# Weight splits ahead of evacuations in the second projection, a residual loaded in four parts, spreading products with 128 rows, a last store from ScalarE: a hybrid mLSTM and stick-breaking layer on one Trainium2 core

## The chip, the cores and the metric

The kernel runs on one core of one Trainium2 chip. The time is the device time of one execution in microseconds (us), the median of several runs. A profile is one execution taken by the hardware profiler; its span goes from the first to the last instruction of the program, and its engines are TensorE (PE; its weight loads are PEld), VectorE (DVE), ScalarE (ACT), GpSimd (POOL) and SyncE (SP). An engine's name with a q (SPq) is its sequencer, which issues transfers and waits for semaphores.

## The reference

One layer over 512 tokens of width 1024, in float32:

```python
h = rmsnorm(x, norm_w)
proj = h @ w_in + b_in            # 1024 -> 11272 columns, split into the parts below
# A: mLSTM, 4 heads of 256: causal conv + SiLU on q and k, matrix memory with gates, per-head norm
y_m = norm(mlstm(mq, mk, mv, mi, mf)) * sigmoid(mo) * silu(mz)
# B: stick-breaking attention, 8 heads of 128, strictly causal, normed q and k
y_s = stick_breaking(norm(sq), norm(sk), sv) * silu(sz)
merged = sigmoid(gm) * (y_m @ w_proj_m) + sigmoid(gs) * (y_s @ w_proj_s)
out = x + merged @ w_out
```

## The kernel before

Every product of two float32 matrices is made of three TensorE products in a faster format: each operand is split into a high half (rounded) and a low half (the rest), and `mm3` (lines 84 to 87) adds high x high, high x low and low x high. ScalarE makes the high half by a copy (line 90), VectorE the low half by a subtraction (line 91).

The program is a list of units, one after the other on TensorE. A unit of a projection is 128 output columns (or 256 input rows) and 24 products of 512 columns each. In order: the input projection (`w_in`), the projection of `y_s` (`w_proj_s`, 8 units), the projection of `y_m` (`w_proj_m`, 8 units, called the second projection), and then the output product. `n_proj` is the number of the first output unit, so units `n_proj - 8` to `n_proj - 1` are the second projection. The heads of both mixers run between the units of the input projection.

The output product is made by a scheme with seven products of half size (numbered 1, 2, 6, 5, 7, 4, 3, in this order) from sums of blocks of `w_out` (B11, B12, B21, B22; T1 to T4 are their sums) and of `merged` (the tables `s`). Each of the seven is two units of 12 products.

For each unit c the main loop (from line 1141) writes the instructions of all engines; each engine then executes its own in that order and waits for the others by semaphores. `ahead(c)` splits the weights of the units up to c + 2 and has SP load the raw weights of the units up to c + 4 (`fetch`). `evac` of unit c - 1 takes its result out of PSUM. `due` is a list of deferred pieces. In the units up to `n_proj` the evacuation comes first, then the deferred pieces, then `ahead`; behind `n_proj` there is an `ahead` in front of the evacuation.

- For the second projection the split is different (`by_dma`, lines 115 to 119): ScalarE copies the high half into `wh` and minus the high half into `wl`, and then GpSimd issues a DMA that adds the raw weight `stg` onto `wl`. The buffers `stg`, `wh` and `wl` have three places each.
- The evacuation of a unit of the second projection (`pm_evac`, lines 850 to 868) is VectorE's product with the gate and sum with the first projection, then ScalarE's copy to `mgh` and VectorE's `mgl`; from the fifth unit on also four VectorE operations for the tables. The evacuation of the first projection is one VectorE operation (line 845).
- `s_turn` splits a table of sums (ScalarE and VectorE), `t4` makes T4 on VectorE.
- `load_xr` (line 932) has SP load the eight 128x512 pieces of x for the residual. It is a deferred piece at unit `n_proj - 2`.
- `add` (line 971) adds a product onto such a piece on VectorE and stores it by SP; the last piece goes in two halves of 256 columns. `add_dma` adds by a DMA from GpSimd.
- Four times, once for each mLSTM head, TensorE spreads a row over all partitions: line 688 multiplies `sel`, a tile of 36 rows with ones in eight of them, with `rb2`, the row in two halves. Both tiles are cleared by GpSimd at the start (lines 496 and 497), then a few rows are written.

Of the kernel before, what the change touches and what calls it, by code (L numbers as in the profile page):

```python
# [9 lines left out]
FR = mybir.dt.float32r  # L10
# [5 lines left out]
T = 512  # L16
# [18 lines left out]
def tile_hybrid_layer(  # L35
# [16 lines left out]
    nc = tc.nc  # L52
    xf = x.flatten_outer_dims()
    of = out.flatten_outer_dims()

    def pool(name, bufs=1, **k):
        return ctx.enter_context(tc.tile_pool(name=name, bufs=bufs, **k))

    cst = pool("cst")
# [13 lines left out]
    def blk(tag, dt=F32, shape=(512,), name=None, p=128):  # L73

        where = mp if tag in MISC else sp
        return where.tile([p] + list(shape), dt, name=name or tag, tag=tag, bufs=BUFS[tag])
# [193 lines left out]
    def x_scale(tb):  # L270
        xs = tiny.tile([128, 4], F32, name="xs", bufs=2)
        ssq, r = xs[:, 0:2], xs[:, 2:3]
        xn = x_t[tb]
        junk = blk("om", BF, (D,), name="junk")
        if tb == 0:
            for i in range(2):
                c = slice(i * D // 2, (i + 1) * D // 2)
                nc.scalar.activation(junk[:, c], xn[:, c], AF.Square, accum_out=ssq[:, i:i + 1])
            nc.gpsimd.tensor_tensor(ssq[:, 0:1], ssq[:, 0:1], ssq[:, 1:2], op=OP.add)
        else:  # L280
            nc.scalar.activation(junk, xn, AF.Square, accum_out=ssq[:, 0:1])
        rstd(r, ssq[:, 0:1], D, EPS)
        nc.vector.tensor_scalar(xn, xn, r, None, op0=OP.mult)

    def x_turn(tb):
        ts = slice(tb * 128, (tb + 1) * 128)
        xn = x_t[tb]
        for g in range(2):
            ks = slice(4 * g, 4 * g + 4)
            tp = att_ps()  # L290
            for j in range(4):
                kt = g * 4 + j
                nc.tensor.transpose(tp[:, j * 128:(j + 1) * 128], xn[:, kt * 128:(kt + 1) * 128], ident)
            dh = hh[:, ks, ts]
            nc.vector.tensor_tensor(dh, tp.rearrange("p (k t) -> p k t", k=4),
                                    nw_t[:, ks].unsqueeze(2).to_broadcast([128, 4, 128]), op=OP.mult)
            for j in range(4):
                k = 4 * g + j
                nc.vector.scalar_tensor_tensor(hl[:, k, ts], tp[:, j * 128:(j + 1) * 128], nw_t[:, k:k + 1],
                                               hh[:, k, ts].bitcast(F32), op0=OP.mult, op1=OP.subtract)  # L300
# [175 lines left out]


    NH = 4
    sel = cst.tile([36, NH, 128], FR, name="sel")
    rb2 = cst.tile([36, T], FR, name="rb2")  # L480
    c_lag = [cst.tile([128, TB, NH], F32, name=f"c_lag{k}") for k in range(TB)]
    em = cst.tile([128, TB, NH], F32, name="em")
    gst = blk("y", shape=(KT, 8), name="gst")
# [3 lines left out]
    def gates_fill():  # L487
        wg = blk("P5", FR, (KT, 128), name="wg")
        nc.gpsimd.memset(wg.bitcast(F32), 0.0)

        sel32 = blk("y", shape=(NH, 128), name="sel32", p=36)
        nc.gpsimd.memset(sel32, 1.0)
        for r in (slice(0, 4), slice(32, 36)):
            nc.gpsimd.affine_select(out=sel32[r], in_=sel32[r], compare_op=OP.is_equal, fill=0.0, base=0,
                                    channel_multiplier=1, pattern=[[-1, 4], [0, 128]])
        nc.gpsimd.memset(sel.bitcast(F32), 0.0)
        nc.gpsimd.memset(rb2.bitcast(F32), 0.0)
        wg_t.extend([wg, sel32])
# [372 lines left out]
    n_proj = len(units)  # L871
# [58 lines left out]

    xr = {}

    def load_xr():
        for n, (g, tb) in enumerate([(0, 0), (0, 1), (1, 0), (1, 1), (1, 2), (1, 3), (0, 2), (0, 3)]):
            tag = ["om", "om", "om", "acc", "tmp", "tmp", "brow", "vh"][n]
            t = blk(tag, shape=({"om": 516, "vh": 576}.get(tag, 512),), name="xr")[:, 0:512]
            nc.sync.dma_start(t, xf[tb * 128:(tb + 1) * 128, g * 512:(g + 1) * 512])
            xr[g, tb] = t
# [32 lines left out]
    def add(g, tb, src, store=False, n=512):  # L971
        t = xr[g, tb]
        for c in range(0, 512, n):
            nc.vector.tensor_tensor(t[:, c:c + n], src[:, c:c + n], t[:, c:c + n], op=OP.add)
            if store:
                nc.sync.dma_start(of[tb * 128:(tb + 1) * 128, g * 512 + c:g * 512 + c + n], t[:, c:c + n])

    def add_dma(g, tb, src):
        nc.gpsimd.dma_start(out=xr[g, tb], in_=src, accum_op=OP.add)
# [10 lines left out]
    def p2():  # L990
        for tb in range(2):
            add(0, tb, bank[2, tb], True)
# [6 lines left out]
    def p5():  # L999
        for tb in range(2):  # L1000
            add(1, 2 + tb, bank[5, tb])
        for tb in range(2):
            add(1, tb, bank[5, tb])
# [27 lines left out]
    def at(c, fn, *a):  # L1031
        later.setdefault(n_proj + c, []).append(lambda: fn(*a))

    for g in range(2):
# [4 lines left out]
        at(-7 + 2 * g, t2, g)  # L1039
        at(-6 + 2 * g, t1, g)  # L1040
        at(1 + g, t4, g)
    at(-2, load_xr)
    for j in range(4):
        at(j // 2, s_turn, 12, j)
        at(3 + j, s_turn, 34, j)
# [89 lines left out]
    def ahead(c):  # L1135
        while count["ready"] < min(N, c + AHEAD + 1):
            fetch(count["ready"] + 1)
            units[count["ready"]].split()
            count["ready"] += 1
        fetch(c + LOADS + 1)  # L1140

    for c in range(N):
        now[0] = c
        if 0 < c < TB:
            ahead(c)
        if c and units[c - 1].slow:
            units[c - 1].slow()
            ahead(c)
        due = later.pop(c, [])
        if c > n_proj:  # L1150
            ahead(c)
        if c:
            units[c - 1].evac()
        for fn in due:
            fn()
        ahead(c)
        units[c].mm(0)
        if c < 2:
            x_turn(c + 1)
        if c == 0:  # L1160
            x_scale(2)
            x_scale(3)
            gates_fill()
        for g in list(act):
            if c in REST:
                continue
            if next(g, "end") == "end":
                act.remove(g)
        for e in list(pend):
            if c >= e[0] and e[2]():  # L1170
                pend.remove(e)
                g = e[3]()
                next(g)
                act.append(g)
        units[c].mm(1)
        if c == 1:
            x_turn(3)
# [31 lines left out]
```

## Time and profile before

| | |
|---|---|
| median of 3 runs | 716.22 us (715.57 to 717.08) |
| the profiled execution | 716.44 us |
| its span | 714.6 us |
| granted TensorE clock over the span | 0.999 |
| TensorE busy | 704.1 us, 3332 products |
| VectorE busy | 446.5 us |
| ScalarE busy | 335.5 us |
| GpSimd busy | 106.8 us |
| moved by DMA | 73.57 MB, of it the accumulating copies and additions (software queue) 5.77 MB |

Each row of a timeline gives the start and the length of an instruction in us, the engine, the line of the kernel, the operation, the tiles as out<-in, and in brackets the idle time of the engine before it and what ended it. `x2` joins two of the same kind in a row. A row of windows gives, for a stretch, its length, the busy time and count of PE, PEld, DVE, ACT and POOL, then the granted clock, the busy share of the 16 DMA engines, and GB/s.

### The profile page before, as it was taken

How to read it: one execution, taken by the hardware profiler on the slowest of the kernel's cores; microseconds unless marked ns; L12 is line 12 of the kernel's file. 1: busy time of each engine (PE TensorE's matmuls, PEld its weight loads, DVE VectorE, ACT ScalarE, POOL GpSimd, SP SyncE). 2: the span in 40 equal slices, each digit the busy share in tenths (PEclk: the TensorE clock that was granted, in tenths of full speed). 3: DMA queues.
4: the chain of work that ended last, by engine and by line, in shares of the span. 5: the costliest groups of instructions: out<-in, count | busy, mean ns of one | idle time of the engine just before them, and what ended most of it. 6: DMA issues, size and time to landing. Idle time of an engine off the chain costs nothing.

```text
span 714.6 us, 9124 instructions
## 1 busy us (share of the span) xinstructions
PE 704.1 (99%) x3332; PEld 586.6 (82%) x3332; DVE 446.5 (62%) x711; ACT 335.5 (47%) x629; POOL 106.8 (15%) x249
## 2 busy tenths in 40 slices
PE   7999999999999999999999999999999999999997
PEld 5888888888888888888888888888888888887786
DVE  6837886656487567279944637995343254445896
ACT  5245364476255544244475534446563253334451
POOL 5412021253022112000001120000111000111010
PEclk9999999999999999999999999999999999999999
DMA  7433332233323222333332233333323236569244
GB/s 241 133 104 93 99 90 73 69 95 87 105 61 88 59 74 75 103 89 90 93 93 79 59 104 89 89 89 89 89 60 87 76 118 222 146 152 263 87 89 117
DMA packets 93492, 73.57 MB, mean 103 GB/s; under 512 B 3694, under 2 KB 77832, under 8 KB 93448
## 3 DMA queue, kind: packets, MB, share of 16 engines
q1 hardware_dynamic: 91432, 67.23, 32.7%
q0 software_dynamic: 2016, 5.77, 4.3%
q8 instruction: 26, 0.43, 0.2%
q14 instruction: 18, 0.15, 0.1%
HBM read 65.12 MB, written 2.10 MB: 94 GB/s over the span
## 4 chain that ended last, share of the span: by engine, by line
PE 88%; issue 5%; DMA 4%; DVE 1%; POOL 1%; SPq 0%; ACT 0%; DVEq 0%; POOLq 0%
PE dps L85 24%; PE dps L87 24%; PE dps L86 24%; PE aps L86 3%; PE aps L87 3%; PE aps L85 3%; DMA wl<-stg 2%; PE aps L447 1%; PE aps L389 1%; PE dps L1098 1%; PE dps L1096 1%; PE dps L1097 1%; DMA stg<-in_w_in_dram 1%; DMA stg<-in_w_proj_m_dram 1%; PE aps L742 1%
## 5 line engine op out<-in xcount | busy, mean ns | idle before, releaser
L91 DVE TENSOR_TENSOR wl<-stg,wh 128x1024 fp32r<-128x1024 f32 x92 | 112.7, 1225 | 124.8 <-ACT wh L90 124.6
L85 PE MATMUL dps<-hh,wh 128*128 128x512 f32 x448 | 175.7, 392 | 0.0
L86 PE MATMUL dps<-hl,wh 128*128 128x512 f32 x448 | 174.5, 390 | 0.0
L87 PE MATMUL dps<-hh,wl 128*128 128x512 f32 x448 | 174.5, 390 | 0.0
L90 ACT ACTIVATE wh<-stg 128x1024 fp32r<-128x1024 f32 x92 | 96.8, 1052 | 63.3 <-PE dps L87 41.1
L85 PEld LDWEIGHTS dps<-hh,wh 128*128 128x128 f32 x448 | 84.1, 188 | 17.7 <-issue 1.0
L87 PEld LDWEIGHTS dps<-hh,wl 128*128 128x128 f32 x448 | 84.1, 188 | 17.7
L86 PEld LDWEIGHTS dps<-hl,wh 128*128 128x128 f32 x448 | 84.1, 188 | 16.6
L85 PE MATMUL dps<-wh,hh 128*128 128x512 f32 x224 | 88.2, 394 | 0.0
L87 PE MATMUL dps<-wh,hl 128*128 128x512 f32 x224 | 87.3, 390 | 0.0
L86 PE MATMUL dps<-wl,hh 128*128 128x512 f32 x224 | 87.3, 390 | 0.0
L87 PEld LDWEIGHTS dps<-wh,hl 128*128 128x128 f32 x224 | 42.0, 188 | 8.9
L85 PEld LDWEIGHTS dps<-wh,hh 128*128 128x128 f32 x224 | 42.1, 188 | 8.3
L86 PEld LDWEIGHTS dps<-wl,hh 128*128 128x128 f32 x224 | 42.1, 188 | 8.2
L633 DVE SCALAR_TENSOR_TENSOR acc<-tmp,vec,acc 128x511 f32<-128x511 f32 (+2 forms) x48 | 36.0, 750 | 1.7
L636 ACT ACTIVATE tmp<-acc 128x512 f32<-128x512 f32 x16 | 10.1, 633 | 50.2 <-DVE acc L633 50.2
L416 POOL TENSOR_SCALAR_AFFINE_SELECT om<-om 128x128 f32<-128x128 f32 x32 | 12.2, 381 | 134.4 <-ACT om L414 134.4
L422 DVE TENSOR_TENSOR_SCAN om<-om 128x512 f32<-128x512 f32 (+3 forms) x32 | 27.9, 871 | 6.3 <-POOL om L416 6.3
L695 POOL TENSOR_SCALAR_AFFINE_SELECT w_all<-om 128x128 f32<-128x128 f32 x16 | 4.1, 296 | 168.9 <-DVE om L690 168.9
L90 ACT ACTIVATE at_split<-aps 128x384 fp32r<-128x384 f32 (+1 forms) x24 | 11.8, 525 | 36.8 <-PE aps L447 36.8
L87 PE MATMUL dps<-yh,wl 128*128 128x512 f32 x64 | 25.2, 394 | 1.1 <-DMA wl<-stg 1.1
L91 DVE TENSOR_TENSOR at_split<-aps,at_split 128x384 fp32r<-128x384 f32 (+1 forms) x24 | 13.7, 599 | 19.8 <-ACT at_split L90 19.8
(273 smaller groups left out, 1248.6 us busy)
## 6 DMA issues: line engine op xcount, KB each, us to landing
stg<-in_w_in_dram SPq DMA_DIRECT2D x87, 512.0 KB, 3.7
stg<-in_w_proj_s_dram SPq DMA_DIRECT2D x8, 512.0 KB, 3.8
B<-in_w_out_dram SPq DMA_DIRECT2D x8, 512.0 KB, 4.6
stg<-in_w_proj_m_dram SPq DMA_DIRECT2D x8, 512.0 KB, 3.6
wl<-stg POOLq DMA_DIRECT2D x8, 512.0 KB, 7.3
brow<-in_b_in_dram SPq DMA_DIRECT2D x8, 256.0 KB, 3.9
xr<-in_x_dram SPq DMA_DIRECT2D x8, 256.0 KB, 7.6
out_dram<-xr SPq DMA_DIRECT2D x7, 256.0 KB, 2.1
```

What stands on the lines that cost most here:

```text
L85: nc.tensor.matmul(ps, ah, bh, start=first, stop=False)
L86: nc.tensor.matmul(ps, ah, bl, start=False, stop=False)
L87: nc.tensor.matmul(ps, al, bh, start=False, stop=last)
L90: nc.scalar.activation(hi, src, AF.Copy)
L91: nc.vector.tensor_tensor(lo, src, hi.bitcast(F32), op=OP.subtract)
L389: nc.tensor.transpose(tp[:, tb * 128:(tb + 1) * 128], self.raw[name][tb][:, hs], ident)
L416: nc.gpsimd.affine_select(out=om[:, ts], in_=om[:, ts], compare_op=OP.is_gt, fill=1.0, base=0, channel_multiplier=1, pattern=[[-1, 128]])
L422: nc.vector.tensor_tensor_scan(back, back, back, 1.0, op0=OP.mult, op1=OP.bypass)
L447: nc.tensor.transpose(tp[:, at + (i - j) * 128:at + (i - j + 1) * 128], a_t[i][:, j * 128:(j + 1) * 128], ident)
L633: nc.vector.scalar_tensor_tensor(acc[:, j:], t[:, 0:T - j], cw(3 - j, ch), acc[:, j:], op0=OP.mult, op1=OP.add)
L636: nc.scalar.activation(t, acc, AF.Sigmoid)
L742: nc.tensor.matmul(nm[:, 0:258], ph, vh, start=j == 0, stop=False)
```

## The change

There are four edits. In the main loop, the `ahead` in front of the evacuation is there from unit `n_proj - 8` on, so for the second projection and the first output unit too. The residual is loaded in four parts of two pieces each, at the units `n_proj - 2`, `n_proj`, `n_proj + 1` and `n_proj + 3`. The tiles `sel` and `rb2` have 128 rows, so that the products of line 688 run over 128 rows; the added rows are zero. The second half of the last stored piece is issued by ScalarE and no longer by SP.

```diff
-    sel = cst.tile([36, NH, 128], FR, name="sel")
-    rb2 = cst.tile([36, T], FR, name="rb2")
+    sel = cst.tile([128, NH, 128], FR, name="sel")
+    rb2 = cst.tile([128, T], FR, name="rb2")
...
-    def load_xr():
+    def load_xr(first):
         for n, (g, tb) in enumerate([(0, 0), (0, 1), (1, 0), (1, 1), (1, 2), (1, 3), (0, 2), (0, 3)]):
+            if n // 2 != first:
+                continue
             tag = ["om", "om", "om", "acc", "tmp", "tmp", "brow", "vh"][n]
...
             if store:
-                nc.sync.dma_start(of[tb * 128:(tb + 1) * 128, g * 512 + c:g * 512 + c + n], t[:, c:c + n])
+                (nc.scalar if c else nc.sync).dma_start(
+                    of[tb * 128:(tb + 1) * 128, g * 512 + c:g * 512 + c + n], t[:, c:c + n])
...
-    at(-2, load_xr)
+    for n, c in enumerate((-2, 0, 1, 3)):
+        at(c, load_xr, n)
...
         due = later.pop(c, [])
-        if c > n_proj:
+        if c > n_proj - 9:
             ahead(c)
         if c:
             units[c - 1].evac()
```

## The prediction

> **What bounds the kernel now.** I read the page first, then TensorE's waits from 30 us on (the start-up is not touched), then the timeline of each engine around the places that the diff names.
>
> ```profile
> span 714.6 us, 9124 instructions
> ...
> PE 704.1 (99%) x3332; PEld 586.6 (82%) x3332; DVE 446.5 (62%) x711; ACT 335.5 (47%) x629; POOL 106.8 (15%) x249
> ```
> ```profile
> PE dps L87 <- DMA wl<-stg: 1.1, 2, 0.7
> PE dps L86 <- DVE wl L91: 0.5, 1, 0.5
> ```
>
> TensorE is the bound: 704.1 of 714.6 us. No product is taken away, so the change can win only what TensorE loses between products. The waits say where: twice for the accumulating copy that finishes the low half of a weight (`wl<-stg`, line 119), once for a subtraction on VectorE. But the waits view counts only idle time. A matmul that starts late still overlaps the one before it (its busy time is about 0.39 us, while a 512-column product starts every 0.23 us), so the loss is read from start times. A block of the second projection is 24 products, and these are the starts of three blocks:
>
> ```profile
> 642.44 0.39 PE L85 MATMUL dps<-yh,wh 128*128 128x512 f32 x1
> ...
> 666.20 0.39 PE L85 MATMUL dps<-yh,wh 128*128 128x512 f32 x1
> ...
> 671.64 0.39 PE L85 MATMUL dps<-wh,mgh 128*128 128x512 f32 x1
> ```
>
> An undisturbed block takes 671.64 - 666.20 = 5.44 us, or 0.227 a product. The five blocks from 642.44 to 671.64 take 29.20 where five times 5.44 is 27.20. **2.00 us are lost in the second projection.**
>
> **Part 1: the split ahead of the evacuation, second projection.** I call a block's start t. At t the loop evacuates the block just ended and splits the weight two blocks ahead: ScalarE copies the high half (line 117) and minus it (118), then GpSimd issues the accumulating copy (119).
>
> ```profile
> 626.09 1.06 ACT L117 ACTIVATE wh<-stg 128x1024 fp32r<-128x1024 f32 x1 [3.43 <-PE dps L86]
> 627.06 1.04 ACT L118 ACTIVATE wl<-stg 128x1024 fp32r<-128x1024 f32 x1
> 633.21 0.63 ACT L857 ACTIVATE mgh<-gm 128x512 fp32r<-128x512 f32 x1 [5.11 <-DVE gm L854]
> 633.75 1.05 ACT L117 ACTIVATE wh<-stg 128x1024 fp32r<-128x1024 f32 x1
> ```
> ```profile
> 628.39 0.86 POOL L119 DMA_DIRECT2D wl<-stg  x1 [4.55 <-ACT wl L118]
> 636.04 0.86 POOL L119 DMA_DIRECT2D wl<-stg  x1 [6.78 <-ACT wl L118]
> ```
> ```profile
> DMA to landing us min/median/max: 5.2/7.7/8.5
> ```
>
> The first row is a block whose evacuation uses no ScalarE: the split starts as soon as TensorE releases the buffer (626.09) and the copy is issued 2.30 later. In the next block ScalarE's queue holds the evacuation's `mgh` first, which waits for two VectorE operations; the split begins at 633.75 instead of 626.09 + 5.44 = 631.53. So the evacuation ahead of it costs each split 2.22 us, and the edit gives these 2.2 back. The low half is needed by the third product of the block two later, t + 2 x 5.44 + 0.45 = t + 11.33. After the change the copy is issued at about t + 2.3, which leaves 9.0 us; the longest copy took 8.5. Before, it was issued at t + 4.5 and had 6.8, less than the median 7.7 (the third fence is the view of the tile `wl` over these blocks). So I take the whole 2.00 as won. It could be nothing, if the copies are held by the DMA engines and not by their issue (a rival below). What is late next: the last weight's copy, with half a microsecond over if it is as slow as the slowest. `mgh` itself moves back by about 0.4 (the two copies, 2.0 after t, instead of the two VectorE operations, 1.5); it is needed by the output products at the earliest several blocks later, except the last ones (part 3). GpSimd has only these copies here; SP's loads keep their order in these blocks and wait for the landings, so they only come earlier.
>
> **Part 2: the residual in four parts.**
>
> ```profile
> 647.15 6.29 SPq L937 DMA_DIRECT2D xr<-in_x_dram  x8
> 654.86 0.38 SPq L892 DMA_DIRECT2D B<-in_w_out_dram  x1
> ```
> ```profile
> 643.20:661.00 17.80, 16.73 (x72) 13.13 (x71) 10.34 (x19) 7.59 (x9) 2.59 (x3) 1.00 1.01 264
> 671.80:694.60 22.80, 22.30 (x98) 18.15 (x98) 22.57 (x35) 14.51 (x24) 3.53 (x4) 1.00 0.22 52
> ```
>
> The eight loads stand in SP's queue ahead of the B21 weights and fall into the stretch where the DMA engines are full (share 1.01) and both late copies fly. Now two of them are queued behind the first B21 load, the other six behind the second. SP waits for nothing else there, so these six go out when the second-to-last copy has landed, some 10 us ahead of the output products; the first user, the addition of the first product, comes two halves of 2.72 us (12 x 0.227) after that product begins. I cost the edit at nothing by itself: it thins the crowd for two copies and moves it onto the last one, which has the 9.0 us above. If that cover is gone, the last block waits for the difference, some tenths.
>
> **Part 3: the split ahead of the evacuation, last two projection blocks and the first output product.** Here the split is by ScalarE and VectorE (lines 90, 91), so the order changes on VectorE too.
>
> ```profile
> 677.08 0.39 PE L85 MATMUL dps<-wh,mgh 128*128 128x512 f32 x1
> 677.96 0.50 PE L86 MATMUL dps<-wl,mgh 128*128 128x512 f32 x1 [0.50 <-DVE wl L91]
> 678.30 0.39 PE L87 MATMUL dps<-wh,mgl 128*128 128x512 f32 x1
> ```
> ```profile
> 671.84 0.69 DVE L853 TENSOR_TENSOR gm<-dps,gm 128x512 f32<-128x512 f32 x1 [0.57 <-PE dps L87]
> ...
> 675.49 1.29 DVE L91 TENSOR_TENSOR s<-gs,s 128x512 fp32r<-128x512 f32 x2
> 676.69 2.35 DVE L91 TENSOR_TENSOR wl<-B,wh 128x1024 fp32r<-128x1024 f32 x2
> 678.96 1.29 DVE L916 TENSOR_TENSOR B<-B,t 128x512 f32<-128x512 f32 x2
> 680.17 1.28 DVE L91 TENSOR_TENSOR s<-gs,s 128x512 fp32r<-128x512 f32 x2
> 681.37 1.29 DVE L91 TENSOR_TENSOR wl<-t,wh 128x512 fp32r<-128x512 f32 x2
> ```
>
> The wait is (677.96 - 677.08 - 0.23) + (678.30 - 677.96 - 0.23) = 0.76 us, for the third weight of the output products, split at 676.69 behind the last evacuation (671.84 to 675.49, 3.65) and two tables (1.20). With the split first, this wait goes. But VectorE is busy 22.57 of the 22.80 us from 671.8 on, and the new order makes it idle while ScalarE makes the high half (1.06 after t). Replayed from t = 0, the first output product: third weight 1.06 to 2.20, evacuation to 5.85, tables to 7.05, fourth weight to 8.27 with TensorE asking at 8.39, then 1.21 and 1.20 of other work, fifth weight begun at 10.60, its first half done at 11.3. TensorE asks for that at 4 x 2.72 + 0.23 = 11.11. So a new wait of 0.2 stands two products later, with 0.1 for starting again (678.30 - 677.96 is 0.34 and not 0.23): the gain is 0.76 - 0.31 = 0.45. Ends: the whole 0.76, or -0.2 if TensorE must have both halves and the fourth weight is late too. I take 0.45, as each step is a row.
>
> **Part 4: 128 rows in the spreading products (line 688).**
>
> ```profile
> 379.74 0.28 PE L87 MATMUL aps<-mqh,mkl 128*128 128x128 f32 x1
> 379.94 0.49 PE L688 MATMUL aps<-rb,sel 36*128 36x512 f32 x1
> 380.37 0.50 PE L85 MATMUL dps<-hh,wh 128*128 128x512 f32 x1
> 380.70 0.39 PE L86 MATMUL dps<-hl,wh 128*128 128x512 f32 x1
> ```
> ```profile
> 359.18 0.18 PEld L688 LDWEIGHTS aps<-rb,sel 36*128 36x128 f32 x1 [0.35 <-issue]
> 359.60 0.19 PEld L85 LDWEIGHTS dps<-hh,wh 128*128 128x128 f32 x1 [0.24 <-issue]
> ```
> ```profile
> L688 PE MATMUL aps<-rb,sel x4: 491/492/492, 359.2 to 506.7; 36*128 36x512 f32 x4
> ```
>
> From 379.74 to 380.70 are 0.96 us where a 128-column and two 512-column products should take 0.11 + 0.23 + 0.23 = 0.57: 0.39 lost around one product of 36 rows. Its weight load and the next one's start with their matmuls instead of ahead of them, so TensorE runs empty on both sides. All four products are alike (491 to 492 ns). With 128 rows they have the shape of their neighbours: 4 x 0.39 = 1.56 won. Ends: nothing, if something else drains TensorE there; no more than 1.56. I take 1.56. By the Trainium skill, "TensorE: Matmul & The Clock Gate", section "Why this matters for your kernels", a product of 32 rows takes the time of one of 128, and rows would change nothing; by "TensorEngine Tiling (Array Packing)", "Key Properties", a change of tiling mode drains TensorE. By the first the sum is 2.5 us, by the second 4.1; the two late weight loads agree with the second. The larger clears of `sel` and `rb2` run on GpSimd at the start, as long as before if they go by columns; nothing on TensorE waits for them until line 688, 300 us later.
>
> **Part 5: the last store.**
>
> ```profile
> 710.71 0.75 DVE L974 TENSOR_TENSOR xr<-aps,xr 128x256 f32<-128x256 f32 x2 [0.19 <-PE aps L87]
> 711.16 0.83 SPq L976 DMA_DIRECT2D out_dram<-xr  x2
> ```
>
> The second half's addition ends at 711.46; SP, still issuing the first half, takes it up around 711.58. ScalarE's queue is empty and could at 711.49: 0.09 won. Its own price is in no row (ScalarE issues no DMA before); GpSimd's copies, the other issuing engine, take 0.86, twice SP's 0.42, so the end is a loss of 0.4. I take 0.09.
>
> **Sum.** 2.00 + 0.45 + 1.56 + 0.09 = 4.10 us. The profiled execution took 716.44 (span 714.6 and 1.8 around it), 0.2 above the median of 716.22. So 712.3 for that execution and 712.1 for the median; I say 712.2, a span near 710.5.
>
> **Rivals.** *The copies are bound by the DMA engines.* For: the share of 1.01, and landings of 7.7 where 5.2 is possible. Against: copies issued one block apart landed in 5.2 to 8.5, so their queue does not grow, and the edit takes six loads out of that stretch. Then the 2.00 stay: 2.10 won, 714.1. *Rows are not the cause*, as the first rule above has it: 2.54 won, 713.7. *Slower: VectorE stuck behind an early split.* At the first output product the split of B21 now stands ahead of the last evacuation; if B21 comes late, evacuation, tables and all further splits wait, one for one, and VectorE has 0.2 us over in the next 22.8. It decides when B21 lands 4.1 us after TensorE reaches the output products; 1.4 more makes the kernel measurably slower, about 718. Against: B21 was issued at 654.86, 17 us ahead. *Nothing happens*, each wait being taken over by a next one: 716.
>
> **Chances.** Forecast (711.3 to 713.2) 0.64; DMA-bound copies 0.13; rows not the cause 0.10; no change 0.08; slower 0.05. I call 0.2% (1.43 us) the least that a measurement here can tell. The first three are faster by that, but for an edge of the second (714.1 against 714.8). Faster 0.86, same 0.10, slower 0.04. The range goes from 711.0 (all waits gone, 0.76 and not 0.45, and a run 0.6 under its median, as 715.57 is) to 714.6, which holds both partial rivals.
>
> **What would show it.** Blocks of the second projection at 5.44 throughout, the copies issued 2.3 after the block's start; line 688 at 0.39 with products 0.23 apart on both sides; no wait at the third output weight, a shorter one at the fifth; TensorE's last product 4.0 earlier. The prediction is wrong if copies take 9 us or more, if TensorE still halts around line 688, if the output products wait more than 0.8, or if ScalarE's store lands later than SP's.

## The result, and the profile after

| | before | after |
|---|---|---|
| median | 716.34 us (6 runs, 715.57 to 717.08) | 712.35 us (6 runs, 711.53 to 712.63) |
| ratio after / before | | 0.9943, 95% interval 0.9930 to 0.9956 |
| profiled execution, span | 716.44, 714.61 us | 712.63, 710.89 us |

The change makes the kernel 4.0 us faster in the medians, 3.73 us in the two spans. From the page of the changed kernel:

```profile
span 710.9 us, 9127 instructions
...
PE 702.3 (99%) x3332; PEld 587.3 (83%) x3332; DVE 446.6 (63%) x711; ACT 335.6 (47%) x629; POOL 107.6 (15%) x249
```

The 3332 products are the same; what shrank is the time between them. Cut at the same instructions in both traces, the spans differ like this:

| stretch | before | after | difference |
|---|---|---|---|
| start to the first spreading product | 359.18 | 359.08 | -0.10 |
| from there to the first projection of the output stage | 223.42 | 222.03 | -1.39 |
| both projections (`w_proj_s`, `w_proj_m`) | 89.04 | 87.04 | -2.00 |
| output product, up to its third product (6) | 11.67 | 11.02 | -0.65 |
| from there to the start of the last matmul | 26.97 | 27.25 | +0.28 |
| from there to the end | 4.33 | 4.46 | +0.13 |

The first row cannot be read: the start-up differs by up to 1.5 us between profiles of this kernel's variants, and of the change it holds only the gap of 0.09 us ahead of that product. The stretches behind it repeat within 0.1 us, so the experiments are read by stretch.

**Second projection.** Block starts, and the copies that finish the weights, in the timelines of the changed kernel's TensorE, ScalarE and GpSimd, and the landings from the view of the tile `wl`:

```profile
640.95 0.39 PE L85 MATMUL dps<-yh,wh 128*128 128x512 f32 x1
...
662.71 0.39 PE L85 MATMUL dps<-yh,wh 128*128 128x512 f32 x1
...
668.15 0.39 PE L85 MATMUL dps<-wh,mgh 128*128 128x512 f32 x1
```
```profile
630.09 1.06 ACT L117 ACTIVATE wh<-stg 128x1024 fp32r<-128x1024 f32 x1 [3.48 <-issue]
631.06 1.04 ACT L118 ACTIVATE wl<-stg 128x1024 fp32r<-128x1024 f32 x1
632.01 0.61 ACT L857 ACTIVATE mgh<-gm 128x512 fp32r<-128x512 f32 x1
```
```profile
626.90 0.86 POOL L119 DMA_DIRECT2D wl<-stg  x1 [4.55 <-ACT wl L118]
632.40 0.86 POOL L119 DMA_DIRECT2D wl<-stg  x1 [4.63 <-ACT wl L118]
```
```profile
DMA to landing us min/median/max: 4.9/6.0/7.4
```

668.15 - 640.95 = 27.20, five times 5.44: no block waits. `mgh` now stands behind the two copies, and the copy on GpSimd is issued 2.3 after `wh` starts, at every block. The copies also became shorter, 6.0 in the median for 7.7.

SP's timeline shows where the residual went, two pieces behind the first B21 load and six behind the second:

```profile
648.92 0.37 SPq L892 DMA_DIRECT2D B<-in_w_out_dram  x1
649.34 0.94 SPq L939 DMA_DIRECT2D xr<-in_x_dram  x2
656.20 0.38 SPq L892 DMA_DIRECT2D B<-in_w_out_dram  x1
656.63 4.41 SPq L939 DMA_DIRECT2D xr<-in_x_dram  x6
```

**Spreading products**, TensorE's matmuls and one weight load:

```profile
379.32 0.28 PE L87 MATMUL aps<-mqh,mkl 128*128 128x128 f32 x1
379.43 0.45 PE L688 MATMUL aps<-rb,sel 128*128 128x512 f32 x1
379.71 0.40 PE L85 MATMUL dps<-hh,wh 128*128 128x512 f32 x1
379.95 0.39 PE L86 MATMUL dps<-hl,wh 128*128 128x512 f32 x1
```
```profile
358.85 0.19 PEld L688 LDWEIGHTS aps<-rb,sel 128*128 128x128 f32 x1
```

From 379.32 to 379.95 are 0.63 us where there were 0.96. The weight load starts ahead of its matmul (358.85 for 359.08). Of the 0.39 lost at this one, 0.055 are left (0.28 from 379.43 to 379.71); two of the four products are like this, the other two are clean.

**Output product.** TensorE and VectorE of the changed kernel:

```profile
676.31 0.39 PE L85 MATMUL dps<-wh,mgh 128*128 128x512 f32 x1
676.54 0.50 PE L86 MATMUL dps<-wl,mgh 128*128 128x512 f32 x1
676.88 0.39 PE L87 MATMUL dps<-wh,mgl 128*128 128x512 f32 x1
...
679.17 0.39 PE L85 MATMUL aps<-wh,s 128*128 128x512 f32 x1
679.55 0.50 PE L86 MATMUL aps<-wl,s 128*128 128x512 f32 x1
679.88 0.40 PE L87 MATMUL aps<-wh,s 128*128 128x512 f32 x1
```
```profile
669.27 1.22 DVE L91 TENSOR_TENSOR wl<-B,wh 128x1024 fp32r<-128x1024 f32 x1 [0.57 <-ACT wh L90]
670.41 0.69 DVE L853 TENSOR_TENSOR gm<-dps,gm 128x512 f32<-128x512 f32 x1
...
674.06 1.29 DVE L91 TENSOR_TENSOR s<-gs,s 128x512 fp32r<-128x512 f32 x2
675.26 1.22 DVE L91 TENSOR_TENSOR wl<-B,wh 128x1024 fp32r<-128x1024 f32 x1
676.40 1.29 DVE L916 TENSOR_TENSOR B<-B,t 128x512 f32<-128x512 f32 x2
677.60 1.29 DVE L91 TENSOR_TENSOR s<-gs,s 128x512 fp32r<-128x512 f32 x2
678.81 1.29 DVE L91 TENSOR_TENSOR wl<-t,wh 128x512 fp32r<-128x512 f32 x2
```

The wait at the third weight (0.79) is gone. Two smaller ones stand in its place: the fourth weight makes its unit 2.86 us long, the fifth makes its unit 3.00, where 2.72 is undisturbed. Together 0.42. At the fourth the subtraction ends at 676.48 and the matmul that needs it starts on the beat, at 676.54, but the next one follows 0.34 and not 0.23 us later. The waits view shows neither, since TensorE is never idle in them: it lists no wait at all between 30 us and the end.

**The end.**

```profile
706.74 0.90 SPq L978 DMA_DIRECT2D out_dram<-xr  x2
706.85 0.76 DVE L976 TENSOR_TENSOR xr<-aps,xr 128x256 f32<-128x256 f32 x2
707.64 0.37 ACTq L978 DMA_DIRECT2D out_dram<-xr  x1
```

ScalarE takes up the last half at 707.64, 0.03 after the addition ends; SP took it up 0.12 after. But the transfer lands 2.05 us after that, where SP's landed 1.95 after, so the two land nearly alike, 3.264 and 3.248 us after the start of the last matmul. The end is 0.13 later.

### The profile page after: what moved, and what is told of

The parts are those of the page before. It is cut to its first block, busy times and chain, and to the rows that moved or that the text cites. A ratio compares the mean times of both kernels' runs of the same rounds, so it can differ in the third digit from the quotient of the medians.

```text
span 710.9 us, 9127 instructions
## 1 busy us (share of the span) xinstructions
PE 702.3 (99%) x3332; PEld 587.3 (83%) x3332; DVE 446.6 (63%) x711; ACT 335.6 (47%) x629; POOL 107.6 (15%) x249
## 4 chain that ended last, share of the span: by engine, by line
PE 97%; DMA 1%; DVE 1%; POOL 0%; SPq 0%; issue 0%; ACT 0%; DVEq 0%
PE dps L85 27%; PE dps L86 27%; PE dps L87 27%; PE aps L86 3%; PE aps L87 3%; PE aps L85 3%; PE aps L447 1%; PE aps L389 1%; PE dps L1102 1%; PE dps L1100 1%; PE dps L1101 1%; DMA stg<-in_w_in_dram 1%; PE aps L742 1%; PE aps L744 1%; PE aps L743 1%; PE aps L769 0%
## 5 line engine op out<-in xcount | busy, mean ns | idle before, releaser
L85 PE MATMUL dps<-yh,wh 128*128 128x512 f32 x64 | 24.9, 389 | 0.0
```

What stands on the lines that cost most here:

```text
L85: nc.tensor.matmul(ps, ah, bh, start=first, stop=False)
```

## The experiments

Each is the changed kernel with the edit shown. Times are read against 712.35 us; the kernel before, timed again beside each run, took 716.41 to 716.75 where it took 716.34.

**The early split undone** (`late_split`).

```diff
-        if c > n_proj - 9:
+        if c > n_proj:
```

> The changed kernel (712.35 us) with the condition of the early split as before (only behind the first output unit). Theory 'issue' (the prediction's): each accumulating copy is issued 4.5 us after its block's start again and has 6.8 us, and the third output weight waits 0.76 us again instead of 0.37; with copies of 5.2 to 8.5 us the 2.00 us in the second projection come back: 714.7 us. Rival 'crowd': the copies were late only because the eight residual loads flew beside them; with the residual in four parts they land in 7 us or less and the blocks lose at most 0.4 us together: 713.1 us. The trace tells it by the five block times up to the output product (27.20 us undisturbed, 29.20 before) and by the landing times.

Measured: 715.11 us median, ratio to the kernel before 0.9978 (0.9962 to 0.9995). In its trace two blocks take 6.57 and 6.14 us, the five together 29.03: 1.83 of the 2.00 are back. TensorE's waits from 600 us on, and the landings:

```profile
PE dps L87 <- DMA wl<-stg: 1.2, 2, 0.8
PE dps L86 <- DVE wl L91: 0.5, 1, 0.5
```
```profile
DMA to landing us min/median/max: 5.5/6.9/8.5
```

The crowd is thinned and copies of 7.8 and 8.5 us still occur; issued 4.5 us into the block, they are late. The first of the two flew beside two residual loads, the second beside six. But such a copy needs no residual load: in the same trace one issued at 626.70, 19 us ahead of the first of them, took 8.0 (issued 2.3 us into its block, it came in time), and in the kernel before the copy issued at 636.04, 11 us ahead of them, took 6.9 and made its block 5.66. The third output unit takes 3.51 us, as before. 'Issue' holds and 'crowd' as the whole cause falls. The twelve runs spread from 712.99 to 718.38, the changed kernel's six from 711.53 to 712.63; whether late copies make this spread is not shown.

**The residual in one part** (`one_load`), and one unit earlier (`xr_first`).

```diff
-    for n, c in enumerate((-2, 0, 1, 3)):
+    for n, c in enumerate((-2, -2, -2, -2)):   # one_load; -3 four times in xr_first
```

> The changed kernel (712.35 us) with all eight residual loads at the unit n_proj - 2 again (behind the first B21 load). Theory 'issue': the copies have 9.0 us, the longest copy took 8.5, so no block waits: 712.35 us, copies of up to 8.5 us. Rival 'crowd': the last two copies fall into the crowd and are over 9 us: 0.5 to 1.8 us more, 712.9 to 714.1 us, seen as blocks over 5.44 us.

> The changed kernel with all eight residual loads a unit earlier, at n_proj - 3, so that SP issues them ahead of the first B21 load, in the order of the kernel before, beside the early split. This is the prediction's own claim on its own: an early issue leaves 9.0 us and the copies that the crowd hit took 8.5 at most before, so no block of the second projection waits: 712.35 us. Rival (after the run with one load, where the last copy took 9.79 us and its block 0.96 longer): the crowd makes some copy longer than 9.0 us wherever it falls, here one of the last three, and 0.3 to 1.8 us are lost.

Measured: 712.39 us (711.89 to 713.04; ratio 0.9936, 0.9920 to 0.9952) and 712.42 us (711.74 to 712.77; 0.9937, 0.9923 to 0.9951). The medians cannot be told from 712.35. The profiled executions can: with one load SP issues the eight in a row, the last copy takes 9.79 us and the last block 6.40 (0.96 lost). Its SP timeline and its waits:

```profile
649.51 0.37 SPq L892 DMA_DIRECT2D B<-in_w_out_dram  x1
649.93 5.45 SPq L939 DMA_DIRECT2D xr<-in_x_dram  x8
656.48 0.38 SPq L892 DMA_DIRECT2D B<-in_w_out_dram  x1
```
```profile
PE dps L87 <- DMA wl<-stg: 0.7, 1, 0.7
```

In `xr_first` the last two copies take 9.35 and 9.26 and one block 5.96 (0.52 lost). The view of `wl` there:

```profile
DMA to landing us min/median/max: 4.9/7.1/9.3
```

So the crowd does make copies longer than the 9.0 us that an early issue leaves. With the residual in four parts and an early split no block waited in any of eight profiled executions (those of the changed kernel and of the seven kernels below that keep both). How often the crowd costs what it cost in these two profiles stays open; on the median it is too little to see.

**Rows** (`rows36`, `rows64`, `rows100`).

```diff
-    sel = cst.tile([128, NH, 128], FR, name="sel")
-    rb2 = cst.tile([128, T], FR, name="rb2")
+    sel = cst.tile([36, NH, 128], FR, name="sel")    # 64 and 100 in the others
+    rb2 = cst.tile([36, T], FR, name="rb2")
```

> The changed kernel (712.35 us) with 36 rows in sel and rb2 again. Theory 'row mode' : TensorE halts 0.39 us around each of the four products: 1.46 us more (the changed kernel still lost 0.055 at two of the four), 713.8 us, and the weight loads of line 688 and of the product behind it start with their matmuls. Rival 'something else drains': no change, 712.35 us.

> The changed kernel with 64 rows in sel and rb2. Theory 'row mode' (TensorE empties where the number of row groups changes): 64 rows are still another mode than 128, so the same loss as with 36: the three start-to-start times from the product before line 688 to the second one behind it sum to 0.964 and 1.080 us, in the changed kernel 0.628 and 0.697. Rival 'every missing row counts' (a loss in proportion): about 0.27 us instead of 0.39 at each.

> The changed kernel with 100 rows in sel and rb2. Theory 'row mode': 100 rows need all four groups of 32, as 128 do, so no loss: 0.628 and 0.697 us as in the changed kernel. Rival 'every missing row counts': about 0.1 us more at each of the four; rival 'only full height': 0.964 and 1.080.

Measured: 714.12 us with 36 rows (713.52 to 714.57; ratio 0.9960, 0.9944 to 0.9976), one run each of 713.91 with 64 and 712.16 with 100. The three start-to-start times around line 688 are 1.080 and 0.964 us with 36 rows, the same to the nanosecond with 64, and 0.703 and 0.639 with 100. The matmuls with 64 rows, then with 100:

```profile
379.60 0.28 PE L87 MATMUL aps<-mqh,mkl 128*128 128x128 f32 x1
379.80 0.49 PE L688 MATMUL aps<-rb,sel 64*128 64x512 f32 x1
380.22 0.50 PE L85 MATMUL dps<-hh,wh 128*128 128x512 f32 x1
380.56 0.39 PE L86 MATMUL dps<-hl,wh 128*128 128x512 f32 x1
```
```profile
378.94 0.28 PE L87 MATMUL aps<-mqh,mkl 128*128 128x128 f32 x1
379.05 0.45 PE L688 MATMUL aps<-rb,sel 100*128 100x512 f32 x1
379.34 0.40 PE L85 MATMUL dps<-hh,wh 128*128 128x512 f32 x1
379.58 0.40 PE L86 MATMUL dps<-hl,wh 128*128 128x512 f32 x1
```

The loss is a step between 64 and 100 rows and not a slope: theory 'row mode'. The Trainium skill, "TensorEngine Tiling (Array Packing)", "Tiling Modes", has modes of 32, 64 and 128 rows and nothing between, and this agrees; the rule of the Trainium skill that the prediction names, "TensorE: Matmul & The Clock Gate", "Why this matters for your kernels", that a product of 32 rows takes the time of one of 128, is about a single product. In this stream 0.34 to 0.38 us are lost around it.

**The last store by SP** (`sp_store`).

```diff
-                (nc.scalar if c else nc.sync).dma_start(
+                nc.sync.dma_start(
```

> The changed kernel (712.35 us) with the last half stored by SP again. Theory: the store from ScalarE is issued 0.09 us earlier, lands 0.02 later against the last matmul, and ScalarE's own closing drain then comes last: from the start of the last matmul to the end 4.47 us in the changed kernel, 4.33 here, so 0.13 us less, below what the timing can tell: read from the profile. Rival: the drain was late by chance: 4.47 here too, or more by the 0.09.

Measured: 712.31 us (711.54 to 712.50; ratio 0.9933, 0.9913 to 0.9952), not told from 712.35. From the start of the last matmul to the end of the span 4.31 us; with ScalarE's store 4.43 to 4.46 in eight profiles, with SP's 4.31 to 4.34 in four, the kernel before among them. The store from ScalarE costs 0.13. In these traces ScalarE's closing drain (one of the last instructions of each engine) comes last: in the changed kernel it runs from 710.53 to 710.67, where VectorE's starts at 710.29 and GpSimd's, the last one where SP stores, ends at 710.54, 0.13 earlier. That this is why is read from the order of the drains and not tested apart.

**The early split only for the second projection** (`dma_blocks`).

```diff
-        if c > n_proj - 9:
+        if n_proj - 9 < c < n_proj - 2 or c > n_proj:
```

> The changed kernel with the early split only where the weight split is one of the second projection (units n_proj - 8 to n_proj - 3), and the old order for the units n_proj - 2 to n_proj. Theory: the second projection keeps its 5.44 us blocks (27.20 for the last five), the third output weight waits 0.79 us as before and the output units behind it wait nothing: 0.37 us more than the changed kernel from the first output product to product 7. Rival: the old order lets the first two residual loads go ahead of the first B21 load, and a copy beside them gets over 9 us: a block over 5.44.

Measured: one run, 712.17 us. Blocks 5.44 throughout; the third output unit takes 3.55, all others 2.72. So in the traces the early split of the last two blocks and the first output unit is worth 0.83 - 0.42 = 0.41 us by itself; the time of one run cannot show it.

**T4 later** (`t4_late`), **and the tables later too** (`best`), both with the last store by SP.

```diff
-        at(1 + g, t4, g)
+        at(5 + g, t4, g)
...
-        at(j // 2, s_turn, 12, j)
+        at(1, s_turn, 12, j)              # best alone
```

> The changed kernel with the last store by SP and T4 made four units later, the tables left as they are. Theory (VectorE's order, step by step as in the prediction's replay): the 0.28 us before product 6 go, since 1.21 us of T4 no longer stand ahead of the fifth weight; the 0.14 us before the fourth weight stay, since nothing ahead of that weight has moved. Rival: the two waits are one backlog that T4 makes, and both go; or neither, if T4 is not what delays the fifth weight.

> The changed kernel with the last store by SP again, T4 made four units later (at n_proj + 5 and + 6) and all four tables of products 6 and 5 split at n_proj + 1, behind the split of the fourth weight's predecessor. Theory: the two waits left in the output product (0.14 and 0.28 us) are VectorE's order alone, and both go: all output units take 2.72 us; with the end 0.15 shorter the time is 0.57 us less, 711.8 us. Rival: VectorE has no time left over in these 23 us, so the work moved out of the way is late elsewhere and another output unit takes over 2.72 us: 712.2 us or more.

Measured: `t4_late` 711.77 us in one run; the fourth output unit takes 2.85, the fifth 2.72: the larger wait went and the smaller stayed. `best` 711.84 us (711.27 to 712.17; ratio 0.9930, 0.9918 to 0.9942); every output unit takes 2.72, and the end 4.34. VectorE's order in `best`:

```profile
673.68 1.22 DVE L91 TENSOR_TENSOR wl<-B,wh 128x1024 fp32r<-128x1024 f32 x1
674.82 2.49 DVE L91 TENSOR_TENSOR s<-gs,s 128x512 fp32r<-128x512 f32 x4
677.23 2.49 DVE L91 TENSOR_TENSOR wl<-t,wh 128x512 fp32r<-128x512 f32 x4
```

The fourth weight directly behind the evacuation, the tables behind it, the fifth and sixth weight in one go. 0.51 us under the changed kernel in the medians where 0.57 was expected. The two intervals overlap, so the gain over the changed kernel is shown by the traces and not by the timing.

## Why the prediction was right

712.2 us was forecast and 712.35 measured, a gain of 4.10 worked out, 3.99 in the medians and 3.73 in the spans. The terms as found come to 3.7, so that the median is only 0.15 off is in part luck: runs of the changed kernel alone spread over 1.1 us. Term by term:

- *Second projection, 2.00 forecast, 2.00 found.* The issue moved from 4.5 to 2.3 us into the block, as worked out, and the run without it lost 1.83. But the step that costed the four-part residual at nothing, "the longest copy took 8.5" against 9.0, failed: the 8.5 was measured with the copies issued late, and with the early issue beside the whole crowd copies take 9.3 to 9.8. Why they are longer there is not shown. Nor was the last copy the one in danger: in the changed kernel it took 5.6, and the one before it, beside the first B21 load and two residual loads, 7.4 (8.5 in `best`, 0.5 short of the 9.0). In the two profiles that keep the crowd 0.52 and 0.96 of the 2.00 come back, though the medians do not show it. The sum was right because both edits were there: the early split carries most of the term, the four parts secure the rest.
- *Output product, 0.45 forecast, 0.37 to 0.41 found.* The replay of VectorE's queue held: the third weight free, the fourth on the edge, the fifth late by a few tenths. The fourth was put 0.12 on the good side (8.27 against 8.39) and was ready only 0.05 ahead; its product starts on the beat, but with the 0.34 behind it the unit loses 0.14, a cost that the replay gave only to a product that comes late. T4 as the work ahead of the fifth weight is shown by moving it.
- *Spreading, 1.56 forecast, 1.44 found*: twice 1.080 - 0.697 and twice 0.964 - 0.628, the same when 36 rows are put back. Most of the missing 0.12 is the 0.055 left at two of the four.
- *Last store, 0.09 less time forecast, 0.13 more found.* This term had the wrong sign. The earlier issue came as worked out, but the landing is 0.10 longer, so the store lands 0.02 later against the last matmul, which the prediction itself names as a sign of being wrong; and the program ends later behind it. No row of before showed either; the bound of a loss up to 0.4 held.
- *The rivals.* DMA-bound copies: no, with an early split and four parts; but a copy's length does depend on what flies beside it. Rows not the cause: no, putting 36 rows back brings the loss back. VectorE stuck: no, ScalarE takes up B21 at 668.17, as soon as TensorE frees the buffer, and waits for no load.

## What to carry to other kernels

Where an engine's queue holds a step that feeds the bottleneck behind one that only empties its results, put the feeding step first, and replay the other engines' queues behind it step by step; the replay here placed the next waits to within 0.15 us. A product with fewer rows than its neighbours can cost a halt on each side, and zero rows that bring it into the same mode took the halt away here at no cost that the traces show (GpSimd's clear of `sel` at the start takes 0.95 us with 36 rows and 0.96 with 128). Read a busy matrix engine by its start-to-start times: 4 us of loss stood in a profile that showed 1.6 us of waits.

## What the runs showed of the hardware that was not expected

- A product of 36 or 64 rows between products of 128 costs 0.34 to 0.38 us more than one of 128, one of 100 rows 0.01.
- An accumulating copy of 512 KB takes 4.6 to 8.0 us beside the loads of weights alone and up to 9.8 with 2 MB of residual loads beside it too, so its latency has to be taken with the transfers that will fly beside it, and not from the old trace.
- The one store from ScalarE makes the program end 0.13 us later, though it starts earlier.
- The twelve runs of the kernel with the late split spread over 5.4 us, the six of the changed kernel over 1.1. In the three longest of the twelve the granted clock was 0.996 to 0.997, for 0.999 to 1.0 in the other nine, which spread over 2.9. No trace of a long run was kept, so whether the late copies cause the spread, or the clock, stays open.
